# A softmax kernel's large loads regrouped: four in place of seven

## The chip, the cores and the metric

One core of one Trainium2 chip. The metric is the device time in microseconds (us) of one execution; each kernel is timed several times beside the kernel before on the same chip. A ratio is the mean time of one kernel's fast runs over that of the other's of the same rounds, so it is not quite the ratio of the medians that are quoted. The profile's span is about 1.85 us shorter than the time.

## The reference

```
x: (16, 1024, 512) float32
x_max = np.max(x, axis=-1, keepdims=True)
exp_x = np.exp(x - x_max)
return (exp_x / np.sum(exp_x, axis=-1, keepdims=True)).astype(np.float32)
```

These are 16384 rows of 512 values, 33.55 MB in and 33.55 MB out. On 128 partitions that makes 128 rows per partition; one "row" below means one row on every partition (2 KB each).

## The kernel before

The rows are cut into chunks. A chunk of R rows is one load; each partition reads R x 2 KB from one unbroken stretch of DRAM (a *run*), and all chunks live in one SBUF tile of 96 rows, at a place that is given with them.

```
CHUNKS = [
    (3, 0), (5, 3), (8, 8), (16, 16), (16, 32), (16, 48), (16, 64), (16, 80), (16, 0), (16, 16),
]                                 # (rows, first row in SBUF)
EARLY = 8                         # loads issued at the start
AFTER_STORE = {2: [8], 3: [9]}    # later loads, after the store of chunk 2, of chunk 3
GROUP = 8                         # rows per reduction
STORE_ROWS = {3: 8, 4: 8, 5: 8}   # rows per store, else the whole chunk
```

Per group of at most 8 rows: VectorE (DVE) finds the maxima, ScalarE (ACT) computes exp and sums row by row, DVE takes reciprocals, scales row by row, and ACT issues the store. Loads are issued by SyncE (SP). DVE reduces the next group before it scales the last, so a reduction that waits for its rows also holds up the scaling and the store behind it.

```
    for g, (k, a, _, _) in enumerate(groups):
        if waiting is not None and a == 0 and k in FINISH_BEFORE:
            scale(waiting); waiting = None
        rowmax(g)                 # DVE, waits for the load
        exps(g)                   # ACT
        if waiting is not None:
            scale(waiting)        # DVE, then the store
        waiting = g
```

Of the kernel before, what the change touches and what calls it, by code (L numbers as in the profile page):

```python
# [1 line left out]

# [4 lines left out]

F32 = mybir.dt.float32
EXP = mybir.ActivationFunctionType.Exp
AX = mybir.AxisListType.X  # L10


CHUNKS = [
    (3, 0), (5, 3), (8, 8), (16, 16), (16, 32), (16, 48), (16, 64), (16, 80), (16, 0), (16, 16),
]
SBUF_ROWS = 96

EARLY = 8
AFTER_STORE = {2: [8], 3: [9]}

GROUP = 8

FINISH_BEFORE = (1, 2, 3)

STORE_ROWS = {3: 8, 4: 8, 5: 8}

ON_ACT = ()

AT_HEAD = {mybir.EngineType.SP: 3}



def loads_at_the_head(nc):

    main, body = nc.main_func.blocks[0], nc.main_func.blocks[1]
    for engine, count in AT_HEAD.items():
        loads = [
            i
            for i in body.instructions
            if i.engine == engine and type(i).__name__ == "InstDMACopy"  # L40
        ][:count]
        barrier = next(
            n
            for n, i in enumerate(main.instructions)
            if i.engine == engine and type(i).__name__ == "InstDrain"
        )
        for load in loads:
            body.instructions.remove(load)
        main.instructions[barrier:barrier] = loads


def one_barrier_on_exit(nc):


    end = nc.main_func.blocks[2].instructions

    def of(engine, kind):
        return [i for i in end if i.engine == engine and type(i).__name__ == kind]

    for engine in (  # L60
        mybir.EngineType.Activation,
        mybir.EngineType.PE,
        mybir.EngineType.DVE,
        mybir.EngineType.SP,
    ):
        arrivals = [i for i in of(engine, "InstDrain") if i.has_update()]
        leaves = of(engine, "InstEventSemaphore")
        assert len(arrivals) == len(leaves) == 2
        end.remove(leaves[0])
        end.remove(arrivals[1])  # L70
    gather, release, gather_2, release_2 = of(mybir.EngineType.Pool, "InstEventSemaphore")
    end.remove(release)
    end.remove(gather_2)

@with_exitstack
def kernel(
    ctx: ExitStack,
    tc: tile.TileContext,
    x: bass.AP,
    out: bass.AP,  # L80
):
    nc = tc.nc
    nc.at_finalize(loads_at_the_head)
    nc.at_finalize(one_barrier_on_exit)
    P = nc.NUM_PARTITIONS

    x_flat = x.flatten_outer_dims()
    out_flat = out.flatten_outer_dims()
    n, d = x_flat.shape
    assert n == P * sum(R for R, _ in CHUNKS)  # L90


    src, dst, at = [], [], 0
    for R, _ in CHUNKS:
        for flat, views in ((x_flat, src), (out_flat, dst)):
            part = flat[at : at + P * R, :]
            views.append(part.rearrange("(p r) d -> p r d", r=R))
        at += P * R

    data = ctx.enter_context(tc.tile_pool(name="data", bufs=1))  # L100
    stats = ctx.enter_context(tc.tile_pool(name="stats", bufs=4))
    held = data.tile([P, SBUF_ROWS, d], F32, name="held")
    place = [held[:, s : s + R, :] for R, s in CHUNKS]


    groups = []
    for k, (R, _) in enumerate(CHUNKS):
        m = -(-R // GROUP)
        cuts = [R * i // m for i in range(m + 1)]
        since = 0  # L110
        for a, b in zip(cuts, cuts[1:]):
            ends = b == R or b - since >= STORE_ROWS.get(k, R)
            groups.append((k, a, b, since if ends else None))
            since = b if ends else since
    shift = [None] * len(groups)
    sums = [None] * len(groups)

    def load(k):
        queue = nc.scalar if k in ON_ACT else nc.sync
        queue.dma_start(out=place[k], in_=src[k])  # L120

    def rowmax(g):
        k, a, b, _ = groups[g]
        shift[g] = stats.tile([P, b - a], F32, name="shift", tag="shift")
        nc.vector.reduce_max(  # L125
            out=shift[g], in_=place[k][:, a:b, :], axis=AX, negate=True
        )

    def exps(g):
        k, a, b, _ = groups[g]  # L130
        sums[g] = stats.tile([P, b - a], F32, name="sums", tag="sums")
        for r in range(a, b):
            nc.scalar.activation(  # L133
                out=place[k][:, r, :],
                in_=place[k][:, r, :],
                func=EXP,
                bias=shift[g][:, r - a : r - a + 1],
                scale=1.0,
                accum_out=sums[g][:, r - a : r - a + 1],
            )  # L140

    def scale(g):
        k, a, b, since = groups[g]
        recip = stats.tile([P, b - a], F32, name="recip", tag="recip")
        nc.vector.reciprocal(out=recip, in_=sums[g])  # L145
        for r in range(a, b):
            nc.vector.tensor_scalar_mul(  # L147
                out=place[k][:, r, :],
                in0=place[k][:, r, :],
                scalar1=recip[:, r - a : r - a + 1],  # L150
            )
        if since is not None:
            nc.scalar.dma_start(
                out=dst[k][:, since:b, :], in_=place[k][:, since:b, :]
            )
        if b == CHUNKS[k][0]:
            for later in AFTER_STORE.get(k, ()):
                load(later)

    with tc.manual_schedule():  # L160
        for k in range(EARLY):
            load(k)
        waiting = None
        for g, (k, a, _, _) in enumerate(groups):
            if waiting is not None and a == 0 and k in FINISH_BEFORE:
                scale(waiting)
                waiting = None
            rowmax(g)
            exps(g)
            if waiting is not None:  # L170
                scale(waiting)
            waiting = g
        scale(waiting)


# [1 line left out]
_INS = ['x']  # L177
_OUTS = [((16, 1024, 512), 'float32')]


# [23 lines left out]
```

## Time and profile before

| | before |
|---|---|
| median time, 3 runs | 161.47 us |
| span | 159.6 us |
| DVE busy, ACT busy | 123.9 us, 93.3 us |
| mean rate over the span | 421 GB/s |
| DVE's waits for loads | 4.6 us, all before the first row |
| issue of the last store | 144.9 us |

Busy time of an engine says little here. The kernel moves a fixed 67.1 MB, and what counts is whether the 16 DMA engines always have work. The trace's packet records hold one record for every run moved by a DMA engine and, for each transfer, 16 four-byte semaphore records, one from each DMA engine that has finished its share.

### The profile page before, as it was taken

What the parts mean: (1) busy time and instruction counts of PE and PEld (TensorE: products, weight loads), DVE (VectorE), ACT (ScalarE), POOL (GpSimd) and SP (SyncE); (2) the same over time, 40 slices, a digit from 0 to 9 for tenths busy, and PEclk for the clock granted to TensorE, in tenths of its full rate; (3) what the DMA queues carried; (4) which work ended last, traced back from release to release, by engine and by line L of the source; (5) the groups of instructions that cost most, each with busy time, mean ns of one, the idle gap of its engine ahead of it and who ended that gap; (6) DMA issues with size and microseconds to landing.
All of it is one profiled execution on the core that took longest, in us unless ns stands there. A gap on an engine that the chain in (4) does not pass through costs nothing.

```text
span 159.6 us, 511 instructions
## 1 busy us (share of the span) xinstructions
DVE 123.9 (78%) x162; ACT 93.3 (58%) x257; POOL 0.2 (0%) x4
## 2 busy tenths in 40 slices
DVE  0482880799699999999999999999999999853000
ACT  0717119207994959595958687776868595940000
POOL 0000000000000000000000000000000000000000
DMA  7999999899999999999899999999999999999993
GB/s 267 443 456 432 399 414 466 375 404 467 411 446 411 485 419 396 439 411 493 378 448 439 411 497 411 405 444 402 435 444 485 411 402 468 435 402 419 485 411 164
DMA packets 3315, 67.13 MB, mean 421 GB/s; under 512 B 368, under 2 KB 368, under 8 KB 624
## 3 DMA queue, kind: packets, MB, share of 16 engines
q1 hardware_dynamic: 1440, 33.56, 49.4%
q10 hardware_dynamic: 1872, 33.56, 49.0%
q14 instruction: 3, 0.02, 0.0%
HBM read 33.55 MB, written 33.55 MB: 421 GB/s over the span
## 4 chain that ended last, share of the span: by engine, by line
DVE 71%; ACT 14%; issue 3%; DMA 3%; DVEq 0%; ACTq 0%
DVE shift L125 39%; DVE held L147 30%; ACT held L133 14%; DMA held<-in_x_dram 3%; DVE recip L145 2%; DVEq L199 0%; ACTq L133 0%
## 5 line engine op out<-in xcount | busy, mean ns | idle before, releaser
L133 ACT ACTIVATE held<-held,shift 128x512 f32<-128x512 f32 x128 | 90.5, 708 | 43.4 <-DVE shift L125 33.3
L125 DVE TENSOR_REDUCE shift<-held 128x8 f32<-128x4096 f32 (+2 forms) x17 | 70.7, 4164 | 4.6 <-DMA held<-in_x_dram 4.6
L147 DVE TENSOR_SCALAR held<-held,recip 128x512 f32<-128x512 f32 x128 | 52.2, 482 | 0.6
L133 ACT ACTIVATION_READ_ACCUMULATOR held<-held,shift 128x1 f32 x128 | 23.9, 187 | 0.0
L145 DVE RECIPROCAL recip<-sums 128x8 f32<-128x8 f32 (+2 forms) x17 | 3.3, 195 | 15.8 <-ACT held L133 15.8
L133 ACT ACT_TABLE_LOAD x1 | 1.3, 1283 | 4.7 <-DMA held<-in_x_dram 4.7
L188 POOL MEMSET const-bfloat16-1.0<- 128x1 bf16 x1 | 0.1, 103 | 0.0
L188 POOL MEMSET const-uint8-127<- 128x1 uint8 x1 | 0.1, 102 | 0.0
L188 POOL MEMSET const-float32-1.0<- 128x1 f32 x1 | 0.1, 100 | 0.0
L188 POOL MEMSET const-float32-0.0<- 128x1 f32 x1 | 0.1, 99 | 0.2 <-issue 0.2
## 6 DMA issues: line engine op xcount, KB each, us to landing
held<-in_x_dram SPq DMA_DIRECT2D x7, 4096.0 KB, 41.8
out_dram<-held ACTq DMA_DIRECT2D x4, 4096.0 KB, 20.9
out_dram<-held ACTq DMA_DIRECT2D x7, 2048.0 KB, 35.3
held<-in_x_dram SPq DMA_DIRECT2D x1, 2048.0 KB, 11.7
held<-in_x_dram SPq DMA_DIRECT2D x1, 1280.0 KB, 7.2
out_dram<-held ACTq DMA_DIRECT2D x1, 1280.0 KB, 19.9
held<-in_x_dram SPq DMA_DIRECT2D x1, 768.0 KB, 4.6
out_dram<-held ACTq DMA_DIRECT2D x1, 768.0 KB, 15.6
```

The source lines that it names most:

```text
L125: nc.vector.reduce_max(out=shift[g], in_=place[k][:, a:b, :], axis=AX, negate=True)
L133: nc.scalar.activation(out=place[k][:, r, :], in_=place[k][:, r, :], func=EXP, bias=shift[g][:, r - a : r - a + 1], scale=1.0, accum_out=s ...
L145: nc.vector.reciprocal(out=recip, in_=sums[g])
L147: nc.vector.tensor_scalar_mul(out=place[k][:, r, :], in0=place[k][:, r, :], scalar1=recip[:, r - a : r - a + 1],)
L188: nc = _bacc.Bacc("TRN2", target_bir_lowering=False, num_devices=1)
```

## The change

Its intent: fewer and larger loads, with longer runs per partition. Which rows a group holds, the order of the groups and the sizes of the 13 stores stay as they were.

```
-CHUNKS = [
-    (3, 0), (5, 3), (8, 8), (16, 16), (16, 32), (16, 48), (16, 64), (16, 80), (16, 0), (16, 16),
-]
+CHUNKS = [(3, 0), (5, 3), (8, 8), (16, 16), (32, 32), (32, 64), (32, 0)]
-EARLY = 8
-AFTER_STORE = {2: [8], 3: [9]}
+EARLY = 6
+AFTER_STORE = {3: [6]}
-STORE_ROWS = {3: 8, 4: 8, 5: 8}
+STORE_ROWS = {3: 8, 4: 8, 5: 16, 6: 16}
```

## The prediction

> **What bounds the kernel now.** I read the page's strip of slices first, then the view of windows, then the DMA view for stretches and for single issues, then DVE's timeline.
>
> ```profile
> DVE 123.9 (78%) x162; ACT 93.3 (58%) x257; POOL 0.2 (0%) x4
> ...
> DVE  0482880799699999999999999999999999853000
> ...
> DMA  7999999899999999999899999999999999999993
> ...
> HBM read 33.55 MB, written 33.55 MB: 421 GB/s over the span
> ```
>
> The DMA engines are full from the first slice to the last; DVE is full only from slice 7 to 34. The chain of waits names DVE for 71% of the span, but its last piece ends at 144.9 us, and 14.7 us of the 159.6 us span follow in which only DMA works. Two stretches, with DMA share and GB/s in the last two columns:
>
> ```profile
> 40.00:100.00 60.00, 58.23 (x80) 45.80 (x129) 0.00 (x0) 1.00 1.00 432
> 110.00:157.00 47.00, 32.25 (x49) 23.43 (x66) 0.00 (x0) 1.00 1.01 434
> ```
>
> So the kernel moves 67.1 MB through a full DMA at 432 to 434 GB/s. Of the span only about 1.0 us before the first packet and the time after the last packet are not transfer. The end, first in windows, then the last scale, the last issue and its us to landing:
>
> ```profile
> 157.00:157.50 0.50, 0.00 (x0) 0.00 (x0) 0.00 (x0) 1.00 0.61 262
> 157.50:158.00 0.50, 0.00 (x0) 0.00 (x0) 0.00 (x0) 1.00 0.01 0
> ...
> 141.64 3.26 DVE L147 TENSOR_SCALAR held<-held,recip 128x512 f32<-128x512 f32 x8
> 144.93 0.34 ACTq L153 DMA_DIRECT2D out_dram<-held  x1
> ...
> out_dram<-held ACTq DMA_DIRECT2D x1, 4096.0 KB, 14.0
> ```
>
> The last 16-row store lands at 158.9, 1.4 us after the last data (157.5). Its own data takes 8 packets per engine of 1.213 us = 9.7 us, so it began at about 147.8. It could have begun at about 145.9 (issue at 144.93 plus the 1.0 us that the first load took from issue to first packet). **DVE may therefore end 1.9 us later before the DMA runs empty.** This slack is the number that decides the case.
>
> How loads (queue q1) and stores (q10) share the engines, from the DMA view of 40 to 100 us:
>
> ```profile
> q1 hardware_dynamic: 591, 17.27, 66.7%
> q10 hardware_dynamic: 592, 8.65, 33.7%
> ```
>
> Equal packet counts, 2:1 in bytes: one packet from each in turn, where a packet is one partition's run (32 KB of a 16-row load, 16 KB of an 8-row store). The trace's packet records have medians of 234, 385, 611 and 1213 ns for 6, 10, 16 and 32 KB and 9 ns for a 4-byte semaphore record.
>
> **What the Trainium skill says.** (1) "DMA: Bandwidth & Descriptors", section Queues, rings and completion order: each DMA engine takes turns between its queues packet by packet. The trace agrees: 591 against 592. (2) Same page, section Where 436 GB/s comes from: 16 ports give 435.2 GB/s. The trace agrees: 434 GB/s with stores alone. (3) Same page, section Why a DMA increments its semaphore by 16 and not by 1: its sentence on rows longer than 64 KiB being cut implies that 64 KiB fits one descriptor. No load of 32 rows (64 KiB per partition) is in this trace, so this is untested here. (4) Same page, section Anatomy of one DMA: most of a transfer's fixed cost is the receipt of the write; the 1.4 us after the last data here agree in kind.
>
> **The change part by part.** Groups, instructions of DVE and ACT, rows in SBUF and the 13 stores with their sizes all stay: 3, 5, 8, six of 8 rows, four of 16. What changes is seven loads becoming four.
>
> *Removed.* Three loads: 3 x 8 = 24 data packets and 3 semaphore records fewer per engine. By the medians, 32 KB costs 602 ns more than 16 KB, so 11 ns of the 1213 are fixed, and about 10 ns x 27 = 0.25 us is saved. I estimate a 64 KB packet at 2 x 1213 - 10 = 2.416 us. This is the whole direct gain.
>
> *Moved: when rows land.* I walk the turns and check the walk on the kernel before. There the first 32 rows land at 24.4 (issue 1.73, 22.7 to landing). The next load's 8 packets of 32 KB meet one 6 KB and seven 10 KB store packets: 8 x 1.213 + 0.234 + 7 x 0.385 = 12.6, so 37.0; measured 2.28 + 34.9 = 37.2. The one after meets one 10 KB and seven 16 KB: 9.7 + 4.7 = 14.4, so 51.6; measured 4.60 + 46.9 = 51.5. The walk holds to 0.2 us. DVE's timeline has its demand for rows 32 and up:
>
> ```profile
> 46.05 4.42 DVE L125 TENSOR_REDUCE shift<-held 128x8 f32<-128x4096 f32 x1
> ```
>
> First 32-row load, after the change: 24.4 + 8 x 2.416 + 0.234 + 7 x 0.385 = **46.7**, against a demand at 46.05: DVE waits 0.7 us, where before its rows had been there since 37.2. All of DVE after it moves by 0.7.
> Second: 46.7 + 19.3 + 4.7 = **70.7**; demand at 77.0 (timeline), now 77.7. No wait.
> Third: it writes rows 0 to 31, so it must wait for the last store of the fourth chunk. Stores get only one turn per 2.4 us, so when the second load is done there are still one packet of the third chunk's store and 16 of the fourth's: 17 x 0.611 = 10.4, so they land at 81.1 (before: the last load was issued at 82.46 for the same reason). From issue to first packet: 1.0 us plus what is queued, which I take as two 16 KB packets, 1.2 us (the first store, issued at 10.17 into a full queue, had its first packet at 13.84). Then 8 x 2.416 + 7 x 0.611 = 23.6, and 1.4 for the receipt: 81.2 + 2.2 + 23.6 + 1.4 = **108.4**. Demand: 107.91 (timeline), now 108.6. It just fits; an error of 1 us in this long sum makes another wait.
> Between 70.7 and 83 the DMA has stores alone, but three more 8-row stores have been issued by 78, so it doesn't run empty.
>
> *On the path.* DVE's end moves by 0.7 us, with the last load perhaps 0.5 more: 0.7 to 1.2. The slack is 1.9, less the 0.25 saved: about 1.6. So DVE's new waits lie beside the full DMA and cost nothing, and the end moves by -0.25 us: 161.47 - 0.25 = 161.2. Where the last load lands 1 us later than I have it, 0.3 to 0.5 us of DMA is lost: 161.6. I put the middle at 161.5.
>
> **The rivals.** *A: larger transfers run faster.* Against it: the stores with 16 KB and 32 KB packets and the mixed stretch differ by 432 to 434 GB/s only, and the fixed part of a packet is 10 ns. It would take 3.2 us to count as faster; 0.25 us is all that larger packets can give. 161.2.
>
> *B: the load is cut into two packets of 32 KB.* Then loads keep their 2:1 share, and the first 32-row load lands when rows 32 to 63 landed before, at 51.5. DVE would wait 51.5 - 46.05 = 5.4 us, pass the slack by 5.4 - 1.9 = 3.5, and the time would be 165.0, 2.2% slower. For it: I only infer that 64 KB fits one packet. Against: the skill's sentence. I give it 1 in 10.
>
> *C: stores starve and the DMA runs empty waiting for the last load's rows.* Its signs would be a hole in the DMA strip near 81 us and DVE waiting at 108. Against: the backlog of stores just counted. It becomes costly only if the last load lands beyond 110, and then 1 us late costs about 1 us: 162 to 164. I give 1 in 6 to a loss of over 1 us this way.
>
> **Range and chances.** The floor is 161.47 - 0.25, less run-to-run scatter of 0.2 to 0.4 us (161.47 to 161.84 before): 160.9. Upwards C gives up to 163.5; B lies beyond, near the line of 2% (164.7). So 161.5, range 160.9 to 163.5. Faster 0.01; slower is most of B and a bad case of C together, 0.1; within 2% 0.89.
>
> **What would show it.** Right: about 0.25 us less DMA work; load packets (q1) 27 x 16 = 432 fewer than 1440, so 1008; a new wait of DVE's reduction for a load of about 0.7 us near 46 and none or a small one near 108; the last load issued at 81 to 82; the DMA strip full until the last slice; loads near 80% of the bytes between 30 and 70 us. Wrong: more load packets than that or a DVE wait of 5 us near 46 (B); empty DMA slices near 81 or before the last store (C); a DVE end later than about 146.5.

## The result and the profile after

The changed kernel takes **164.22 us** (median of 6 runs, 164.04 to 164.98) against 161.45 for the kernel before (6 runs, 161.40 to 161.84). The ratio is 1.0174, with a 95% interval of 1.0152 to 1.0195: 2.8 us slower, and outside the predicted range.

The page of the changed kernel: the strips of DVE and DMA in 40 slices, the HBM line and the chain of waits.

```profile
DVE  0491960899649999999999999992999999958000
...
DMA  7999998979898898899999899797999999996996
...
HBM read 33.55 MB, written 33.55 MB: 414 GB/s over the span
...
DMA 63%; DVE 19%; ACT 5%; issue 3%; SPq 0%; DVEq 0%; ACTq 0%
```

The DMA strip has a 6 in the fourth slice from the end, where before it was full. DVE has two new holes (the 4 in slice 12 and the 2 in slice 28). The chain, which ran over DVE before, now runs over loads and stores for 63% of the span. DVE's timeline names the holes; the last bracket is its idle time and what ended it:

```profile
48.28 4.42 DVE L123 TENSOR_REDUCE shift<-held 128x8 f32<-128x4096 f32 x1 [2.35 <-DMA held<-in_x_dram]
...
113.23 4.42 DVE L123 TENSOR_REDUCE shift<-held 128x8 f32<-128x4096 f32 x1 [3.02 <-DMA held<-in_x_dram]
```

The first wait is for the first load of 32 rows, the second for the last. They hold DVE up by 5.4 us, and the last store is issued at 150.24 instead of 144.93. The timeline has the issue, and the DMA view of that moment its us to landing:

```profile
150.24 0.34 ACTq L151 DMA_DIRECT2D out_dram<-held  x1
```

```profile
out_dram<-held ACTq DMA_DIRECT2D x1, 4096.0 KB, 11.1
```

Three windows around it (the last two columns are DMA share and GB/s; the view books a packet whole where it starts, so the share can pass 1 and falls about one packet too early):

```profile
148.00:149.00 1.00, 1.00 (x4) 0.00 (x0) 0.00 (x0) 1.00 0.38 164
149.00:151.00 2.00, 1.21 (x4) 0.00 (x0) 0.00 (x0) 1.00 0.12 49
151.00:160.00 9.00, 0.00 (x0) 0.00 (x0) 0.00 (x0) 1.00 1.09 466
```

By the packet records the DMA engines are busy 89% of the time from 148 to 149, 34% from 149 to 150 and 12% from 150 to 151: for two microseconds most of them have nothing to do. The last store has 11.1 us from issue to landing, where it had 14.0 when it stood in a queue. Its first packet comes at 151.08 (packet records), 0.84 us after the issue.

The turns between the queues are as predicted. The DMA view of 30 to 70 us has 235 load packets (q1) against 249 store packets (q10), but loads now carry 81% of the bytes (13.63 of 16.76 MB); the last column is the share of the DMA engines' time:

```profile
q1 hardware_dynamic: 235, 13.63, 80.4%
q10 hardware_dynamic: 249, 3.13, 18.3%
```

The whole run has 1008 load packets instead of 1440, as predicted, and the packet of 64 KB has a median of 2.418 us. Yet the DMA engines did not get less work: all packet times together are 158.4 us per DMA engine, against 157.0 in the kernel before, because many packets took longer than the median. What the prediction did not see either is in the semaphore records: the DMA engines end the first 32-row load between 45.6 and 47.9 us, 2.3 us apart, and the last store but one between 148.6 and 151.3, 2.7 us apart.

### The profile page after: what moved, and what is told of

Read it like the earlier page. It is cut to its first block, busy times and chain, and to the rows that moved or that the text cites. A ratio compares the mean times of both kernels' runs of the same rounds, so it can differ in the third digit from the quotient of the medians.

```text
span 162.2 us, 505 instructions
## 1 busy us (share of the span) xinstructions
DVE 124.1 (76%) x162; ACT 93.3 (57%) x257; POOL 0.2 (0%) x4
## 3 DMA queue, kind: packets, MB, share of 16 engines
q1 hardware_dynamic: 1008, 33.55, 49.2%
## 4 chain that ended last, share of the span: by engine, by line
DMA 63%; DVE 19%; ACT 5%; issue 3%; SPq 0%; DVEq 0%; ACTq 0%
DMA held<-in_x_dram 47%; DMA out_dram<-held 16%; DVE shift L123 11%; DVE held L145 8%; ACT held L131 5%; DVE recip L143 0%; SPq L118 0%; DVEq L197 0%; ACTq L131 0%
```

## The experiments

Theory W, formed on this profile: DVE's two waits push the last issue beyond what the full DMA hides. Rival M: the DMA itself does worse with loads of 32 rows. A third idea, R, came out of the first runs: a load that starts when no other load is queued (the load queue is *dry*) costs DMA time. The edits below are cut to the lines that matter (`...` marks a cut); where EARLY, AFTER_STORE or STORE_ROWS are left out, they follow so that the stores keep their sizes and each load waits for the stores that free its rows.

All results at a glance. "Apart" is the distance between the first and the last DMA engine's record of the last store but one, that is, after all loads and before the end.

| kernel | DVE waits after the first load, us | last issue, us | apart, us | median, us | ratio (95%) |
|---|---|---|---|---|---|
| before | 0 | 144.9 | 1.2 | 161.45 | 1 |
| changed | 2.4 + 3.0 | 150.2 | 2.7 | 164.22 | 1.0174 (1.0152 to 1.0195) |
| last chunk split | 2.2 | 146.9 | 4.1 | 165.44 | 1.0243 (1.0228 to 1.0259) |
| first chunk split | 5.4 | 150.1 | 2.3 | 163.90 | 1.0147 (1.0131 to 1.0163) |
| only the middle at 32 | 0 | 145.0 | 2.2 | 162.93 | 1.0079 (1.0061 to 1.0097) |
| first two in runs of 32 KB | 5.4 | 150.1 | 1.3 | 163.88 | 1.0148 (1.0133 to 1.0163) |
| before, idle DVE work of 2.3 us | 0 | 146.9 | 1.3 | 161.57 | 1.0009 (0.9992 to 1.0025) |
| before, idle DVE work of 5.6 us | 0 | 150.3 | 1.4 | 163.94 | 1.0155 (1.0139 to 1.0170) |
| before, late load, failed | 0 | 144.9 | 1.2 | 161.42 | 1.0001 (0.9986 to 1.0016) |
| middle at 32, not dry | 3.3 | 148.1 | 2.2 | 162.49 | 1.0064 (1.0049 to 1.0079) |
| before, load queue dry | 0 | 144.7 | 0.8 | 161.99 | 1.0033 (1.0018 to 1.0048) |
| two loads per chunk | 0 | 144.8 | 1.3 | 161.45 | 0.9994 (0.9978 to 1.0011) |
| fifth chunk stored by 16 | 2.3 + 8.2 | 155.5 | 0.2 | 169.30 | 1.0480 (1.0459 to 1.0501) |
| middle at 32, runs of 32 KB | 3.5 | 148.3 | 1.4 | 161.92 | 1.0024 (1.0008 to 1.0041) |

(In the run with the fifth chunk stored by 16 the wait of 8.2 us leaves the DMA engines empty and so brings them together again ahead of the store but one; it had 1 round, the other experiments 3.)

**The last chunk as two loads of 16.**

```
-... (32, 32), (32, 64), (32, 0)]            AFTER_STORE = {3: [6]}
+... (32, 32), (32, 64), (16, 0), (16, 16)]  AFTER_STORE = {2: [6], 3: [7]}
```

> The last 32-row chunk is two loads of 16 rows again; the first two 32-row loads stay. Theory W (DVE's two waits for 32-row loads, 2.35 us at 46 and 3.0 us at 110, push its end beyond a slack of about 2.9 us): the wait at 110 goes, because rows 0 to 15 only wait for the stores of the first three chunks (landed at 72.5) and are loaded by about 95; the wait at 46 stays; the last issue is at about 147.2, inside the slack: 161.3 to 161.9 us. Rival M (the DMA itself moves 64 KB packets less well, so it is longer in proportion to the rows loaded in them): two thirds of the loss stays, about 163.3 us.

Measured: 165.44 us, the opposite of W and more than M. The second wait is gone and the last issue is at 146.9, as W had it. Still this kernel is 1.2 us slower than the changed one. Its windows at the end (DMA share and GB/s last):

```profile
157.00:158.00 1.00, 0.00 (x0) 0.00 (x0) 0.00 (x0) 1.00 1.14 492
158.00:159.00 1.00, 0.00 (x0) 0.00 (x0) 0.00 (x0) 1.00 0.31 131
159.00:160.00 1.00, 0.00 (x0) 0.00 (x0) 0.00 (x0) 1.00 0.15 66
160.00:161.00 1.00, 0.00 (x0) 0.00 (x0) 0.00 (x0) 1.00 0.08 33
161.00:162.00 1.00, 0.00 (x0) 0.00 (x0) 0.00 (x0) 1.00 0.08 33
```

The DMA runs out slowly: a share of 0.08 to 0.15 is one or two of 16 engines starting a packet. Most are done at 158.2 to 159.3 us; the last record is at 162.3. Nobody waits for anything but these. So W cannot be the whole story: DMA engines that are late with their share set the end here.

**The first chunk as two loads of 16.**

```
-... (32, 32), (32, 64), (32, 0)]            EARLY = 6
+... (16, 32), (16, 48), (32, 64), (32, 0)]  EARLY = 7   (the last load still after chunk 3's store)
```

> The first 32-row chunk is two loads of 16 again; the second and third stay at 32. Theory W: no wait at 46 (rows land at 37 and 51); the last load is issued at 81 to 83, as its store of the fourth chunk allows, lands about 30 us later at 112, against a demand that is now at 108: one wait of 3.5 to 5 us, last issue at 148.5 to 150, about 1 to 2 us past the slack: 162.3 to 163.5 us. Rival M: about 163.3 us as well, so this run is for the waits; under M no relation between the wait and the time.

Measured: 163.90 us. The wait at 46 is gone. The last load is issued at 81.76, and DVE waits longer for it, because DVE asks earlier:

```profile
113.05 4.42 DVE L123 TENSOR_REDUCE shift<-held 128x8 f32<-128x4096 f32 x1 [5.36 <-DMA held<-in_x_dram]
```

The last issue is at 150.1, as in the changed kernel, and the time is close to it too. Both are slightly above what W expected. The middle load has runs of 64 KB here, and its DMA engines ended only 1.4 us apart; the 2.3 us of the table arose around the last load.

**Only the middle chunk at 32 rows.**

```
-... (32, 32), (32, 64), (32, 0)]
+... (16, 32), (16, 48), (32, 64), (16, 0), (16, 16)]   (EARLY = 7, AFTER_STORE = {2: [7], 3: [8]})
```

> Only the middle chunk has 32 rows; the first and the last are two loads of 16. Theory W: that load has seven us to spare and nobody waits for it: no wait of DVE after the first load, last issue at 144.8, 161.3 to 161.6 us like the kernel before. Rival M: one third of the loss, about 162.4 us.

Measured: 162.93 us, so W alone fails: no wait, last issue at 145.0, and still 1.5 us slower. The end again:

```profile
157.00:158.00 1.00, 0.00 (x0) 0.00 (x0) 0.00 (x0) 1.00 0.99 426
158.00:159.00 1.00, 0.00 (x0) 0.00 (x0) 0.00 (x0) 1.00 0.23 98
159.00:160.00 1.00, 0.00 (x0) 0.00 (x0) 0.00 (x0) 1.00 0.08 33
```

Fifteen of the 16 engines are done about 1.0 us later than before (158.3 to 159.3 instead of 157.3 to 158.4), and the last ends at 160.5 instead of 158.5. These are two different losses. The second arises at the 32-row load: the two loads ahead of it have their engines 1.1 us apart, this one 2.2 us (74.5 to 76.7), and so have the last six stores. The first sits near 97 us. There the last load was issued at 92.34, after the load before it had landed (91.6), and had its first packet only at 96.66. In the ten microseconds from 95 the packets took, summed per DMA engine, 0.84 us more than the medians for their sizes; in the kernel before it was 0.02 in that stretch.

**The first two 32-row loads in runs of 32 KB.** Each of the two chunks lies in two blocks of 16 SBUF rows that do not touch, so one transfer of 32 rows moves twice as many runs of half the size.

```
+    blocks = held.rearrange("p (b r) d -> p b r d", r=16)
+    apart = {4: blocks[:, 2:5:2], 5: blocks[:, 3:6:2]}
...
-        queue.dma_start(out=place[k], in_=src[k])
+        queue.dma_start(out=apart[k], in_=src[k].rearrange("p (b r) d -> p b r d", r=16))   # chunks 4, 5
...                             (reductions, exp, scales and stores address the rows the same way)
```

> The changed kernel, with the first two 32-row chunks each in two blocks of 16 rows of SBUF that do not touch, so that each is still one load of 32 rows but in runs of 32 KB. Theory W with turns packet by packet: loads fall back to two thirds of the bytes, the first 32-row load lands at about 51.7 and DVE waits 5.5 to 6 us there; the last load is issued at about 82 to 83 and lands at 113, by when DVE (demand at 113.5) waits little or not at all; last issue at about 150 to 151: 164 to 165 us, the same time as the changed kernel by another wait. Rival M: with a third of the 64 KB packets the time falls to about 162.4 us.

Measured: 163.88 us, and the wait is where the turns packet by packet put it:

```profile
51.26 4.42 DVE L141 TENSOR_REDUCE shift<-held 128x8 f32<-128x4096 f32 x1 [5.39 <-DMA held<-in_x_dram]
```

With runs of 32 KB the first 32-row load lands at 51.2, with runs of 64 KB at 48.3: the share of a queue follows the length of its runs. Both these loads leave the engines 1.3 us apart, where the changed kernel has 2.3 and 2.2. The last issue is at 150.1, and the time is that of the other kernels that issue at 150: with DVE as late as in the changed kernel, engines that stay together gain only 0.3 us.

**The kernel before with DVE made late.** An idle reduction of rows that nobody needs, ahead of the 14th group; nothing of the DMA traffic is changed.

```
+            if g == 13:
...
+                nc.vector.reduce_max(out=spare[:, 0:4], in_=place[4][:, 0:4, :], axis=AX, negate=True)
             rowmax(g)
```

> The kernel before with one idle reduction of 4 rows (about 2.3 us by the reductions of 3 and 5 rows) put in on DVE ahead of the 14th group. It measures how late DVE may be. Theory T (the time is the later of two ends: last issue plus 0.9 us plus the last store's 9.7 us, or the DMA engine that is last with its share) expects the last issue at 147.2, hidden behind the late DMA engines: 161.3 to 161.7. The prediction's slack of 1.9 us expects 161.8. A rival that DVE's delay always costs expects 163.7.

Measured: 161.57 us, ratio 1.0009 (0.9992 to 1.0025). The reduction takes 2.28 us, the last issue is at 146.93, 2.0 us later than before, and no loss is seen.

The second run has reductions of 8 and of 2 rows at the same place.

> The kernel before with idle reductions of 8 and of 2 rows (about 5.5 us) at the same place: as late as the changed kernel's DVE, without any 32-row load. Theory T: last issue at 150.4, data until 161.0, all DMA engines empty for 2 to 3 us ahead of it, 163.8 to 164.2 us, like the changed kernel. If what costs the changed kernel is its DMA traffic and not DVE, this stays below 163.

Measured: 163.94 us. The two reductions take 5.6 us. The last issue in the timeline, and windows ahead of it:

```profile
150.33 0.34 ACTq L153 DMA_DIRECT2D out_dram<-held  x1
```

```profile
147.00:148.00 1.00, 0.96 (x4) 0.00 (x0) 0.00 (x0) 1.00 0.38 164
148.00:149.00 1.00, 1.00 (x3) 0.00 (x0) 0.00 (x0) 1.00 0.00 0
149.00:151.00 2.00, 1.29 (x4) 0.00 (x0) 0.00 (x0) 1.00 0.00 0
```

A late DVE alone, with every load as before, gives the changed kernel's time within 0.3 us and a hole in the DMA ahead of the last store, as there (here most engines stop at 147.8, in the changed kernel at 149.1). DVE is 5.4 us later and the time 2.5 us longer, so about 2.9 us of lateness are free. The medians of the kernels that issue last at 150.1 to 150.3 are 163.88 to 164.22, the issue plus 13.6 to 14.0 us; 148.3 gives 161.92 and 155.5 gives 169.30, plus 13.6 and 13.8. One kernel falls out: 148.1 gives 162.49, plus 14.4 (the run with the middle at 32 and not dry, below), where the last DMA engine ends the store before only at 150.1.

**A load that starts into stores alone.** The first attempt only moved the last load in program order, behind the fifth chunk's store:

```
-AFTER_STORE = {2: [8], 3: [9]}
+AFTER_STORE = {2: [8], 4: [9]}
```

> The kernel before with its last 16-row load issued after the fifth chunk's store instead of the fourth's: the load queue is empty for some microseconds near 100 us, and no load has 32 rows; the rows land at about 121, before DVE asks for them at 123.4. Theory R (a load that starts into stores alone costs every DMA engine about 0.8 us, as the packet records of four of the kernels with 32-row loads show): 162.0 to 162.5 us without any wait of DVE. Rival S (the loss without DVE waits comes from runs of 64 KB alone): 161.3 to 161.7.

Measured: 161.42 us, and it is no test. The load goes to SBUF rows 16 to 31, so it waits for the fourth chunk's stores wherever it stands; it was issued at 82.43, as before. In the second attempt it goes to rows that the fifth chunk leaves:

```
-... (16, 80), (16, 0), (16, 16)]
+... (16, 80), (16, 0), (16, 32)]   (and AFTER_STORE as above)
```

> The run meant to empty the load queue did not, because the load waited only for the fourth chunk's stores wherever it stood. Here the last 16-row load goes to SBUF rows 32 to 47 and so has to wait for the fifth chunk's stores: issued about 101.5, first packet about 4 us later, landed about 121.5, before DVE asks at 123.4. No load has 32 rows. Theory R (a load that starts into stores alone costs each DMA engine 0.7 to 0.8 us): 162.1 to 162.4. Rival S (only runs of 64 KB cost): 161.3 to 161.7.

Measured: 161.99 us, ratio 1.0033 (1.0018 to 1.0048). The load is issued at 100.67, has its first packet at 104.97 and lands in time. From 100 to 110 us the packets take 0.97 us per DMA engine over their medians (before: 0.02). All engines are done at 158.3 to 159.1 instead of 157.3 to 158.5; the last one loses least, because the engines are also closer together. So R is seen with loads of 16 rows too, and costs 0.5 us here; the expected 0.6 to 0.9 was a little too much.

The counterpart takes this cost out of the run with the middle chunk at 32. The fourth chunk is stored in one piece, so that its store needs half the turns:

```
-STORE_ROWS = {3: 8, 4: 8, 5: 8, 6: 16}
+STORE_ROWS = {4: 8, 5: 8, 6: 16}
```

> The run with only the middle chunk at 32 rows, with the fourth chunk stored in one piece of 16 rows, so that these stores take half as many turns and land about 82 instead of 92, while the 16-row load before the last is still queued: the load queue never runs empty. Theory R: the 0.8 us go, 162.0 to 162.3, and what is left is one or two late DMA engines. Rival S: unchanged, 162.9.

Measured: 162.49 us. The last load is issued while the one before it is queued, and the packets between 70 and 110 us take no longer than their medians, as R has it. But this run has a wait that I had not foreseen: with store runs of 32 KB the 32-row load itself gets fewer bytes and lands late, and DVE waits 3.3 us at 80. The time is thus no clean measure of R. The engines are 2.2 us apart from the 32-row load on, as in the run without this, and the last one sets the end (159.8; most are done at 158.8).

**The middle chunk at 32 rows in runs of 32 KB.** As above for the first two, here for the middle one:

```
+    apart = {6: blocks[:, 3:6:2]}    (the 16-row chunk ahead of it at SBUF row 64)
```

> The run with only the middle chunk at 32 rows, with that load in two blocks of SBUF that do not touch, so in runs of 32 KB. Theory L (runs of 64 KB push DMA engines apart: 2.2 us between first and last after that load, against 1.2 to 1.3 with 16-row loads): the spread stays 1.2 to 1.4 through to the end. The load lands at about 80.5, DVE waits 3.4 us at 77, the last issue is at about 148.4, the last record at about 159.2, 161.9 to 162.3 us; the stores of the fourth chunk land while the next load is still queued, so no restart is paid. If the rows of the load and not its runs push the engines apart, the spread is 2 us or more and the time 162.5 to 163.5.

Measured: 161.92 us, with the expected wait (3.5 us), last issue (148.3) and last record (159.1). The engines leave the 32-row load 1.4 us apart and stay so. In this pair of runs it is the run length of 64 KB and not the 32 rows that drives them apart, and the first two 32-row loads above agree. Against the run before this one, which issues its last store at the same moment within 0.2 us and restarts no load either, the time is 0.6 us shorter (ratios to the kernel before of 1.0024 and 1.0064): about what the late engines cost there. (The two also differ in how the fourth chunk is stored, so this is not quite a clean pair.)

**Two loads per 32-row chunk.** The changed kernel with its chunks and stores, where only the loads are halved:

```
+        for i in range(0, R, 16):
+            if part is None or part == i // 16:
+                n = min(16, R - i)
...                                 (dma_start of rows i to i + n)
-AFTER_STORE = {3: [6]}
+AFTER_STORE = {2: [(6, 0)], 3: [(6, 1)]}    (chunk 6, first and second half)
```

> The changed kernel with its 32-row chunks and its stores as they are, but each 32-row chunk loaded by two transfers of 16 rows (runs of 32 KB, every second one of the chunk), the first half of the last chunk after the third chunk's store. Only the size of the loads is undone; where rows lie in DRAM and the stores' pitch of 64 KB stay. If the load size is the whole cause, everything is as before: no wait of DVE after the first load, spread between first and last DMA engine about 1.2 us, 161.3 to 161.7. If the layout of the 32-row chunks in DRAM costs something, it is longer by that.

Measured: 161.45 us, ratio 0.9994 (0.9978 to 1.0011). The view of waits has the start alone, in one piece:

```profile
DVE shift L129 <- DMA held<-in_x_dram: 4.4, 1, 4.4
```

With loads of 16 rows everything is as before, though the rows lie in DRAM as in the changed kernel and the stores have its pitch. So the loads of 32 rows, with their moments of issue, are the whole cause.

**The fifth chunk stored by 16 rows.**

```
-STORE_ROWS = {3: 8, 4: 8, 5: 16, 6: 16}
+STORE_ROWS = {3: 8, 4: 16, 5: 16, 6: 16}
```

> The changed kernel with the fifth chunk stored in pieces of 16 rows (runs of 32 KB instead of 16). It is for the 4.6 us from the last load's issue (82.7) to its first packet, where the prediction had 2.2: if the load stands behind a fixed number of store packets, about seven, the first packet comes about 8 to 9 us after the issue; if behind a fixed amount of data or time, 4 to 5 us. Then the load takes turns with 32 KB packets, 8 x (2.42 + 1.21) = 29 us, and lands at about 117 to 121: DVE waits 7 to 11 us and the time is 168 to 172 us.

Measured: 169.30 us, with a wait of 8.2 us for the last load. It is issued at 82.74 and has its first packet at 87.42, 4.7 us later, with store runs of 32 KB; in the changed kernel it was 4.5 us (82.68 to 87.21) with runs of 16 KB. A fixed number of packets ahead of it is excluded. In the kernels where the load queue is dry this delay is 3.7 to 4.7 us.

## Why the prediction was wrong

**The DMA's own saving shows in the medians alone.** 1008 load packets, 2.418 us for 64 KB (estimate 2.416), one packet from each queue in turn, one run of 64 KB per packet: these were right. Rival B is excluded, and so is A. But the sum of all packet times did not fall by 0.25 us per DMA engine, it rose by 1.35 (157.03 to 158.38; the four traces with the loads of the kernel before and no dry queue lie within 157.03 and 157.31). Between 80 and 95 us alone, around the start of the last load, the packets took 0.96 us more than their medians (before: 0.00).

**The step that failed** is "DVE's new waits lie beside the full DMA and cost nothing, and the end moves by -0.25 us". DVE's end moved by 5.3 us, not by 0.7 to 1.2. Its terms:

- *First 32-row load, 46.7.* Measured 48.3, a wait of 2.35 us instead of 0.7. The walk carried on from the landing of the load before, with DMA engines 1.1 us apart, as if that distance would stay. It became 2.3 us, and a load lands after its last engine (47.9). In runs of 32 KB the same load ends 1.3 us apart. The other 0.4 us are that all engines took longer: the first one needed 22.8 us where the walk has 22.3.
- *Last 32-row load, 108.4.* Measured 113.2. Of the 4.8 us, 1.5 are the later issue (82.68 instead of 81.2), 2.3 the time from issue to first packet (4.5 us instead of 2.2), and 1.0 the rest (26.0 us from first packet to landing instead of 25.0). The second is the largest: I took the DMA to start a new load behind two store packets, though the prediction itself quotes a start that took 3.7 us, that of the first store (10.17 to 13.84).
- *Slack, 1.9.* Too small, not too large: 2.0 us of lateness cost nothing, and 5.4 us cost 2.5, so it is 2.9. I had measured it on a typical DMA engine (147.8), while in the kernel before the last engine starts its last store about 1.1 us later. The 1.4 us "after the last data" come from the same misreading: the window view books a packet where it starts, and by the packet records the last data is at 158.5 and not at 157.5. So 1.0 us of the 1.4 is the distance between a typical engine and the last, and the landing itself 0.34.

Two small slips change nothing: by the medians quoted the fixed part of a packet is 9 ns and not 11, and DVE's strip is full from slice 12 and not 7.

With the measured terms the prediction's own sum works: 5.3 - 2.9 = 2.4 us, against 2.7 us in the span of the profiled run and 2.8 us in the medians. Rival C described this outcome, a last load beyond 110 and 162 to 164 us, and I gave it 1 in 6. Of its signs, the hole near 81 did not come, where stores wait in plenty; the one ahead of the last store did.

**What the prediction did not have at all** are late DMA engines. The run with the last chunk split has no DVE lateness beyond the slack and is the slowest of the four runs made together, because its last DMA engine ends 3.7 us after that of the kernel before (162.3 against 158.5). In the changed kernel both ends fall together: its late DVE lets the last store begin at 151.1, and its last DMA engine finishes the store before at 151.3 and could not begin earlier either. So it has two causes, and by these two numbers each would have been enough. The late DVE alone is shown to give 163.94, and 163.88 with the changed kernel's loads where most of them keep the engines together; late engines, with the restart of a dry load queue, are shown to give 162.93 and 165.44. Removing the second wait, as the first theory asked, did not help. No run takes both waits and nothing else out of the changed kernel.

**What stays open.** Why runs of 64 KB drive the DMA engines apart is not settled. The first load with such runs left them 2.1 to 2.3 us apart in five kernels, but 1.4 in the run with the first chunk split and 1.3 in the run whose last load alone had such runs, so it does not happen each time. Nor is it settled why a load into a queue of stores takes 3.7 to 4.7 us to begin and then mostly costs 0.8 to 1.1 us of packet time per DMA engine: in the run with the first two loads in runs of 32 KB the packets after such a start took no longer than usual, and after the second such start of the run with the last chunk split only 0.2 us longer. No variant beat the kernel before; the best, two loads per chunk, is the same.

## What to carry to other kernels

When the DMA is full, an idle compute engine is free only up to a slack, and this can be measured directly by adding idle work: here 2 us cost nothing and 5.4 us cost 2.5. A larger load lands later for its first row, waits for more stores before it may be issued, and leaves its queue dry more easily; the packets it saves were worth 0.25 us by their medians, and the sum of packet times grew all the same. Look at the first and the last DMA engine of a transfer, not at their mean: a mean share near 1 hides one engine that is microseconds behind, and the end is the end of that one.

## What the Trainium skill lacked or had wrong

- "DMA: Bandwidth & Descriptors", section Specifications, gives about 0.6 us to the first byte for transfers issued from SP or ACT. Into an empty DMA the runs show 0.84 to 1.05 us from issue to first packet; for a load into one that is busy with stores, 3.7 to 4.7 us. The page has no figure for the second.
- "SBUF — State Buffer", section The DMA setup-cost knee, says to coalesce into the largest single transfer one can. Here the step from 4 MB to 8 MB per load saved 0.25 us of DMA work by the packets' medians, raised the sum of packet times by 1.35 us per DMA engine and lost 2.8 us in all, through landing times and DMA engines that are apart.
- No page has a figure for how far apart the 16 DMA engines of a transfer end, or says that this distance stays while the DMA is full: 0.9 to 1.2 us in the kernel before, 2.2 to 4.1 us ahead of the last store in most kernels with runs of 64 KB, and 0.2 us after the DMA had run empty.
